# Local attention: the gate projected with its columns on the partitions, two blocks of rows moving

## The chip, the cores and the metric

One Trainium2 chip, one of its cores. The metric is device time in microseconds of one execution, from start to end. Three runs of the kernel before gave 1719.83, 1720.24 and 1720.41 us; the median is 1720.24.

## The reference

One decoder layer on x, 4096 rows of 1024, in float32. One input projection gives the columns of two branches. Branch A is attention over a sliding window of 128 rows with 8 query heads and 2 key heads of 64, a sink per head and partial rotary; branch B is a chunked gated linear attention. Each branch has a gate path.

```python
proj = jnp.einsum('bsd,de->bse', x, w_in[layer])
q_a, k_a, v_a, g_a, q_b, k_b, v_b, g_b, r_b = split_cols(proj, IN_SPLITS)
out_a = sliding_window_attention(q_a, k_a, v_a, attn_sinks[layer]) * jax.nn.silu(g_a)
...
mix = jnp.einsum('bse,ed->bsd', jnp.concatenate([out_a, out_b], axis=-1), w_out[layer])
x = layer_norm(ALPHA * x + mix, ln_g[layer], ln_b[layer])
```

The change is about `silu(g_a)`: 512 gate columns for each row, which multiply branch A's output.

## The kernel before

x is cut into 32 blocks of 128 rows and lies in HBM with its columns first, so that a block in SBUF has 128 of the 1024 columns on the partitions, in eight slices k. Every float32 operand of a product is split into a rounded high part and the low rest (`split`, line 97), and each product is made of three matmuls: high by high, high by low, low by high (`project`, lines 142 to 144). There x is the stationary operand, 128 by 128, and the weights move, up to 512 columns; the result has rows on the partitions.

The program has three stages. Stage A (lines 147 to 485) is the local attention: for each block n the queries `pq`, keys and values `pkv`, the gate `pg`, the scores `psc`, and the output. It keeps two steps under way: in the turn of block n, `a_out(n-1)` is worked off in five pieces between the parts of block n's gate projection. Its output `att` is made with the columns on the partitions, since the next stage wants it so, but the gate has rows there, so `a_out` ends with four transposes of the gate (`tg`, line 430) and a product on VectorE (line 431). The order of the pieces is: `turn(0)` and `turn(1)` (transposes of the probabilities `pt`, split into `hl`, and four selects on GpSimd each, into `p`), `mul(0)`, `mul(1)` (four matmuls `po` each), and the gate's product. In between, `a_turn_k` and `a_turn_q` transpose keys (`tk`) and queries (`tq`). The gate's activation (`a_gate`, line 315) is called after the last piece. Stage B (495 to 770) is the linear attention, and stage C (773 on) the output projection `py` and the layer norm. What A and B make goes through HBM (`mixd`) into C.

x is loaded and split by `load_x` (line 127) one block ahead, on GpSimd (high part) and VectorE (low part). Its tiles `xraw`, `xh` and `xl`, two of each, belong to the pool `xp`, which lives through all stages: stage C uses the same tiles for the rows of `mixd` (`mr`, `mh`, `ml`).

Pools are stacked in SBUF. Those of a stage are given back at its end, and the next stage's pools begin at the same place. Stage B's first pool is `wrb`, three raw weight tiles of 2 KB per partition, used for the output weights in the last block; stage C's first is `c1`, whose first tile, `lg` of 4 KB, lies where the first two of these lay. A tile may be written when all that overlaps it has been read.

Matmul results lie in PSUM banks, two of each tag. The order of each engine's instructions isn't quite the program's: when the program is built, a scheduler goes through each engine's instructions by priority in program order, takes the first whose inputs and tiles are ready by its own estimate of times, and so fills gaps with later work. On the chip each engine then keeps this order, and SyncE's queue of DMA issues too.

The start (lines 150 to 210) loads and splits x of blocks 0 and 1 and the weights of queries, keys and values; the gate's weights follow at line 459, through six raw tiles (`wra`). Blocks 0 and 30 project the queries and keys of two blocks (`both`).

Of the kernel before, what the change touches and what calls it, by code (L numbers as in the profile page):

```python
# [9 lines left out]
F32 = mybir.dt.float32  # L10
F32R = mybir.dt.float32r
# [39 lines left out]
def layer_kernel(  # L51
# [74 lines left out]

    def load_x(n, heng, leng):
        raw = xp.tile([P, NK, P], F32, tag="xraw", name=f"xraw{n}")
        sp.dma_start(raw, xt[n])
        h = xp.tile([P, NK, P], F32R, tag="xh", name=f"xh{n}")  # L130
        l = xp.tile([P, NK, P], F32R, tag="xl", name=f"xl{n}")
        for q in range(2):
            s = slice(4 * q, 4 * q + 4)
            split(h[:, s], l[:, s], raw[:, s], heng, leng)
        return h, l

    def project(dst, x, wg, n, k0=0, k1=NK):

        hs, ls = wg
        for k in range(k0, k1):  # L140
# [3 lines left out]
            pe.matmul(dst[:, :n], b, hs[k][:, :n], start=False, stop=(k == NK - 1))  # L144


    with ExitStack() as pa:
        e1 = pa.enter_context(tc.tile_pool(name="e1", bufs=1))
        wr = pa.enter_context(tc.tile_pool(name="wra", bufs=6))
        with ExitStack() as pstart:  # L150
# [12 lines left out]
            for m in range(2):  # L163
                raws.append(xp.tile([P, NK, P], F32, tag="xraw", name=f"xraw{m}"))
                xs.append(tuple(xp.tile([P, NK, P], F32R, tag=t, name=f"{t}{m}") for t in ("xh", "xl")))
            w = []
            for c in range(4):
                s = slice(2 * c, 2 * c + 2)
                for m in range(2):
                    sp.dma_start(raws[m][:, s], xt[m][:, s])  # L170
                    w.append(load_chunk(ws, w_a, 2 * c + m, 0, 512, 0, 512))
            w += [load_chunk(ws, w_a, k, 512, 256, 1, 272) for k in range(NK)]
            posi = e1.tile([P, NB], I32, tag="posi", name="posi")
            sp.dma_start(posi, pos)
            for c in range(4):
                s = slice(2 * c, 2 * c + 2)
                for m in range(2):
                    split(xs[m][0][:, s], xs[m][1][:, s], raws[m][:, s], act, dve)
                    split(*w[2 * c + m], act, dve)
# [3 lines left out]

            posf = e1.tile([P, NB], F32, tag="posf", name="posf")
            dve.tensor_copy(posf, posi)
            freq = e1.tile([P, HALF], F32, tag="freq", name="freq")
# [4 lines left out]
            ang = e1.tile([P, NB, HALF], F32, tag="ang", name="ang")  # L191
            t1 = e1.tile([P, NB, HALF], F32, tag="t1", name="t1")
            dve.tensor_tensor(
# [104 lines left out]
        def a_turn_q(n, qk):  # L298

            tq = bank("tp", f"tq{n}")  # L300
            for j in range(4):
                pe.transpose(
                    tq[:, j * P : (j + 1) * P],
                    qk[:, 2 * j : 2 * j + 2, :].rearrange("p h d -> p (h d)"),
                    ident,
                )
            qs = e2.tile([P, 8, P], F32R, tag="qs", name=f"qs{n}")
            tqv = tq.rearrange("p (j s) -> p j s", j=4)
            act.copy(qs[:64, :4, :], tqv[:64])
            dve.tensor_tensor(qs[64:, :4, :], tqv[:64], qs[:64, :4, :], ALU.subtract)  # L310
            act.copy(qs[:64, 4:, :], tqv[64:])
            dve.tensor_tensor(qs[64:, 4:, :], tqv[64:], qs[:64, 4:, :], ALU.subtract)
            return qs

        def a_gate(n, pg):
            sg = a2.tile([P, 512], F32, tag="sg", name=f"sg{n}")
            tanh[0] = act.activation(sg, pg, AF.Tanh, scale=0.5)
            dve.scalar_tensor_tensor(sg, sg, 1.0, pg, ALU.add, ALU.mult)
            return sg

        def a_scores(n, qs):
# [13 lines left out]
            for g in range(2):  # L335
# [23 lines left out]
                dve.tensor_tensor(es[:, gs], ngm[:, gs], snk[:, gs], ALU.add)  # L359
                pr = a4.tile([P, 4, P], F32, tag="pr", name=f"pr{n}_{g}")  # L360
                for i in range(4):
# [10 lines left out]

        def a_out(n, pn, sg):

# [61 lines left out]

        scores, sg, wb, qks, kks = None, None, {}, {}, {}
        for n in range(NB):
            last = n == NB - 1
            if 0 < n < NB - 1:  # L440
                xs.append(load_x(n + 1, pool, dve))
            both = n in (0, NB - 2)
            group = [n, n + 1] if both else [] if n in (1, NB - 1) else [n]
            pqs = [bank("pj", f"pq{m}") for m in group]
            for i in range(4):
                for m, pq in zip(group, pqs):
                    project(pq, xs[m], wq, 512, 2 * i, 2 * i + 2)
                if scores:
                    pn = next(scores)
# [12 lines left out]
            if n == 2:  # L462
                wb["k"] = load_group(wr, w_b, 272, 256, 3, 256)
            po = a_out(n - 1, pn, sg) if n > 0 else iter(())
# [4 lines left out]
            project(pg, xs[n], wg, 512, 3, 6)  # L469
            next(po, None)  # L470
            a_turn_k(n, kks[n])
            project(pg, xs[n], wg, 512, 6, 7)
            qs = a_turn_q(n, qks[n])
            project(pg, xs[n], wg, 512, 7, 8)
# [9 lines left out]
        for _ in a_out(NB - 1, pn, sg):  # L484
            pass
# [8 lines left out]

    with ExitStack() as pb:
        wr = pb.enter_context(tc.tile_pool(name="wrb", bufs=3))
        f1 = pb.enter_context(tc.tile_pool(name="f1", bufs=1))
        f2 = pb.enter_context(tc.tile_pool(name="f2", bufs=2))
        b1 = pb.enter_context(tc.tile_pool(name="b1", bufs=1))
        b2 = pb.enter_context(tc.tile_pool(name="b2", bufs=2))  # L500

        am = [b1.tile([P, 4, P], F32, tag=f"am{i}", name=f"am{i}") for i in range(2)]
        qbh = [b1.tile([P, 2, 2, P], F32R, tag=f"qbh{i}", name=f"qbh{i}") for i in range(2)]
# [222 lines left out]
        for n in range(NB):  # L726
            x, last = bx_next, n == NB - 1
            if not last:
                bx_next = load_x(n + 1, pool, dve)
            pq = bank("pj", f"bq{n}")  # L730
# [41 lines left out]

    with ExitStack() as pcx:
        c1 = pcx.enter_context(tc.tile_pool(name="c1", bufs=1))
        c2 = pcx.enter_context(tc.tile_pool(name="c2", bufs=2))
# [4 lines left out]
        for n in range(NB):  # L780
            raw = xp.tile([P, NK, P], F32, tag="xraw", name=f"mr{n}")
            sp.dma_start(raw[:, :4, :], mixd[n][0])
            sp.dma_start(raw[:, 4:, :], mixd[n][1])
            xr = c2.tile([P, D], F32, tag="xr", name=f"xr{n}")
            sp.dma_start(xr, xn[n * P : (n + 1) * P, :])
            mh = xp.tile([P, NK, P], F32R, tag="xh", name=f"mh{n}")
            ml = xp.tile([P, NK, P], F32R, tag="xl", name=f"ml{n}")
            split(mh, ml, raw, act, dve)
            y = c2.tile([P, D], F32, tag="y", name=f"y{n}")
# [108 lines left out]
```

## Time and profile before

| what | value |
|---|---|
| median of 3 runs | 1720.24 us |
| the profiled execution | 1719.78 us |
| its span, first to last instruction | 1718.1 us |
| mean granted TensorE clock | 0.997 |
| DMA, mean over the span | 70 GB/s |

The profile is of one execution of its own. Engines are named PE (TensorE's matmuls), PEld (its weight loads), DVE (VectorE), ACT (ScalarE), POOL (GpSimd) and SP (SyncE). A row gives the line of the kernel, the operation and the tiles it writes and reads (`out<-in`, buffer numbers left out). Matmuls are pipelined: one of 512 columns shows 0.39 us, but the next starts 0.23 us later, so on TensorE starts are compared, not durations. An arrow in brackets says who ended an idle time.

### The profile page before, as it was taken

What the parts mean: (1) busy time and instruction counts of PE and PEld (TensorE: products, weight loads), DVE (VectorE), ACT (ScalarE), POOL (GpSimd) and SP (SyncE); (2) the same over time, 40 slices, a digit from 0 to 9 for tenths busy, and PEclk for the clock granted to TensorE, in tenths of its full rate; (3) what the DMA queues carried; (4) which work ended last, traced back from release to release, by engine and by line L of the source; (5) the groups of instructions that cost most, each with busy time, mean ns of one, the idle gap of its engine ahead of it and who ended that gap; (6) DMA issues with size and microseconds to landing.
All of it is one profiled execution on the core that took longest, in us unless ns stands there. A gap on an engine that the chain in (4) does not pass through costs nothing.

```text
span 1718.1 us, 26157 instructions
## 1 busy us (share of the span) xinstructions
PE 1689.6 (98%) x9477; PEld 1445.5 (84%) x9477; DVE 1123.9 (65%) x2562; ACT 774.8 (45%) x2070; POOL 486.6 (28%) x623
## 2 busy tenths in 40 slices
PE   8999999999999998999999999999999899999998
PEld 7788888888888886888888888888888788888886
DVE  7777777777777786666666666666665755555555
ACT  6444344444344455555555555555555522222221
POOL 1333223333223355222222222222222422222221
PEclk9999999999999999999999999999999999999999
DMA  6211111111111131111111111111111444444442
GB/s 221 70 38 38 48 46 38 38 37 38 49 45 38 38 110 63 45 38 38 38 38 38 38 38 38 38 38 38 38 38 38 154 147 147 145 142 142 148 147 86
DMA packets 66389, 119.68 MB, mean 70 GB/s; under 512 B 22738, under 2 KB 27220, under 8 KB 66260
## 3 DMA queue, kind: packets, MB, share of 16 engines
q1 hardware_dynamic: 66260, 118.01, 21.6%
q8 instruction: 74, 1.21, 0.3%
q14 instruction: 55, 0.45, 0.1%
HBM read 84.37 MB, written 33.62 MB: 69 GB/s over the span
## 4 chain that ended last, share of the span: by engine, by line
PE 58%; DVE 1%; ACT 0%; issue 0%; POOL 0%; DVEq 0%
PE py L142 7%; PE py L144 7%; PE py L143 7%; PE bg L142 3%; PE bg L144 3%; PE bv L142 3%; PE bv L143 3%; PE bg L143 3%; PE bv L144 3%; PE bq L142 2%; PE bq L143 2%; PE bq L144 2%; PE bk L144 2%; PE bk L143 2%; PE bk L142 2%; PE to L719 1%
## 5 line engine op out<-in xcount | busy, mean ns | idle before, releaser
L394 POOL TENSOR_SCALAR_AFFINE_SELECT p<-hl 128x512 fp32r<-128x512 f32 x256 | 165.2, 681 | 385.9 <-ACT hl L388 351.7
L142 PE MATMUL py<-wh,mh 128*128 128x512 f32 x512 | 199.8, 390 | 0.0
L143 PE MATMUL py<-wl,mh 128*128 128x512 f32 x512 | 199.7, 390 | 0.0
L144 PE MATMUL py<-wh,ml 128*128 128x512 f32 x512 | 199.4, 390 | 0.0
L363 ACT ACTIVATE pr<-psc,ngm 128x128 f32<-128x128 f32 x256 | 90.5, 366 | 196.0 <-PE psc L344 138.1
L813 POOL TENSOR_TENSOR y<-y,lg 128x1024 f32<-128x1024 f32 x31 | 74.2, 2392 | 267.9 <-ACT y L812 267.9
L567 POOL TENSOR_TENSOR qp<-bqs,ee 128x256 f32<-128x256 f32 x32 | 23.7, 740 | 337.4 <-ACT ee L564 323.4
L144 PEld LDWEIGHTS py<-wh,ml 128*128 128x128 f32 x512 | 96.4, 188 | 20.1
L143 PEld LDWEIGHTS py<-wl,mh 128*128 128x128 f32 x512 | 96.4, 188 | 19.8
L142 PEld LDWEIGHTS py<-wh,mh 128*128 128x128 f32 x512 | 96.4, 188 | 19.7
L142 PE MATMUL pg<-wh,xh 128*128 128x512 f32 x256 | 110.8, 433 | 1.5 <-ACT wh L100 1.5
L142 PE MATMUL bg<-wh,xh 128*128 128x512 f32 x256 | 107.3, 419 | 0.0
L142 PE MATMUL bv<-wh,xh 128*128 128x512 f32 x256 | 103.8, 405 | 0.0
L100 ACT CAST mh<-mr 128x1024 fp32r<-128x1024 f32 x32 | 33.7, 1053 | 154.2 <-PE py L143 154.2
L142 PE MATMUL pq<-wh,xh 128*128 128x512 f32 x256 | 103.2, 404 | 0.0
L144 PE MATMUL bg<-wh,xl 128*128 128x512 f32 x256 | 101.2, 395 | 0.0
L144 PE MATMUL pg<-wh,xl 128*128 128x512 f32 x256 | 101.0, 395 | 0.0
L144 PE MATMUL pq<-wh,xl 128*128 128x512 f32 x256 | 101.0, 395 | 0.0
L143 PE MATMUL bv<-wl,xh 128*128 128x512 f32 x256 | 101.0, 395 | 0.0
L143 PE MATMUL bg<-wl,xh 128*128 128x512 f32 x256 | 100.8, 394 | 0.0
L143 PE MATMUL pq<-wl,xh 128*128 128x512 f32 x256 | 100.7, 393 | 0.0
L143 PE MATMUL pg<-wl,xh 128*128 128x512 f32 x256 | 100.3, 392 | 0.2 <-DVE wl L105 0.2
(225 smaller groups left out, 4897.1 us busy)
## 6 DMA issues: line engine op xcount, KB each, us to landing
xraw<-in_xt_dram SPq DMA_DIRECT2D x62, 512.0 KB
mr<-mx SPq DMA_DIRECT2D x64, 256.0 KB
xr<-in_xn_dram SPq DMA_DIRECT2D x32, 512.0 KB
out_dram<-y SPq DMA_DIRECT2D x31, 512.0 KB
mx<-att SPq DMA_DIRECT2D x32, 256.0 KB
mx<-mb SPq DMA_DIRECT2D x32, 256.0 KB
wraw<-in_w_a_dram SPq DMA_DIRECT2D x16, 256.0 KB
wraw<-in_w_b_dram SPq DMA_DIRECT2D x16, 256.0 KB
```

What stands on the lines that cost most here:

```text
L100: act.copy(hdst, src)
L142: pe.matmul(dst[:, :n], a, hs[k][:, :n], start=(k == 0), stop=False)
L143: pe.matmul(dst[:, :n], a, ls[k][:, :n], start=False, stop=False)
L144: pe.matmul(dst[:, :n], b, hs[k][:, :n], start=False, stop=(k == NK - 1))
L363: act.activation(pr[:, i], sc[i], AF.Exp, bias=ngm[:, h : h + 1], scale=0.125, accum_out=den[:, h : h + 1])
L394: pool.affine_select(o, hl[:, i], [[0, 4], [sg_, P]], ALU.is_gt if b else ALU.is_ge, 0.0, base=0, channel_multiplier=-sg_,)
L567: pool.tensor_tensor(qp, B[n]["q"], ee, ALU.mult)
L719: pe.transpose(to[:, hs], og[:, hs], ident)
L813: pool.tensor_tensor(y, y, lg, ALU.mult)
```

## The change

Stage A's x is held in tiles of two blocks, so that 256 rows lie side by side. The gate's weights become the stationary operand, 128 columns at a time, and x moves, 256 rows of a pair; the result has the columns on the partitions. The even block of a pair projects gate columns 0 to 255 for both blocks, the odd one the rest. The four transposes go, and the product reads the gate from SBUF. The activation is called before the product. The gate's weights are loaded in two halves of columns. To make room, x's tiles no longer live through all stages: each stage has its own, and only two raw tiles of half a block (`xw`) are common; `wra` has three tiles for six, and some tiles move between pools (`pr`, `qs`, start-up tiles).

```diff
-    xp = ctx.enter_context(tc.tile_pool(name="xp", bufs=2))
+    xw = ctx.enter_context(tc.tile_pool(name="xw", bufs=2))
...
+    def one_block(xp, n):
+        t = xp.tile([P, 2, NK, P], F32R, tag="xhl", name=f"xhl{n}")
+        return t[:, 0], t[:, 1]
+
+    def load_halves(wr, src, c0, slot):
+        hs, ls = ([wp.tile([P, 512], F32R, tag=f"w{t}{slot}_{k}", name=f"w{t}{slot}_{k}") for k in range(NK)] for t in "hl")
+        for i in range(2):
+            c = slice(256 * i, 256 * i + 256)
+            for k in range(0, NK, 2):
+                raw = wr.tile([P, 512], F32, tag="wraw", name=f"wraw{slot}_{k}_{i}")
+                for j in range(2):
+                    r = raw[:, 256 * j : 256 * j + 256]
+                    sp.dma_start(r, src[k + j, :, c0 + 256 * i : c0 + 256 * i + 256])
+                    split(hs[k + j][:, c], ls[k + j][:, c], r, act, dve)
+        return hs, ls
...
-    def load_x(n, heng, leng):
-        raw = xp.tile([P, NK, P], F32, tag="xraw", name=f"xraw{n}")
-        sp.dma_start(raw, xt[n])
-        h = xp.tile([P, NK, P], F32R, tag="xh", name=f"xh{n}")
-        l = xp.tile([P, NK, P], F32R, tag="xl", name=f"xl{n}")
+    def load_x(n, parts, heng, leng):
+        h, l = parts
         for q in range(2):
             s = slice(4 * q, 4 * q + 4)
-            split(h[:, s], l[:, s], raw[:, s], heng, leng)
+            raw = xw.tile([P, 4, P], F32, tag="xraw", name=f"xraw{n}_{q}")
+            sp.dma_start(raw, xt[n][:, s])
+            split(h[:, s], l[:, s], raw, heng, leng)
...
+    def project_turned(dst, x, wg, cols, k0=0, k1=NK):
+        hs, ls = wg
+        for k in range(k0, k1):
+            a, b = (t[:, k].rearrange("p m s -> p (m s)") for t in x)
+            for i, c in enumerate(cols):
+                o = dst[:, 256 * i : 256 * i + 256]
+                c = slice(c * P, (c + 1) * P)
+                pe.matmul(o, hs[k][:, c], a, start=(k == 0 and i == 0), stop=False)
+                pe.matmul(o, hs[k][:, c], b, start=False, stop=False)
+                pe.matmul(o, ls[k][:, c], a, start=False, stop=(k == NK - 1 and i == 1))
...
+        xa = pa.enter_context(tc.tile_pool(name="xa", bufs=2))
+        xpair = []
+        def half_pair(n):
+            if n % 2 == 0:
+                t = xa.tile([P, 2, NK, 2, P], F32R, tag="xhl", name=f"xhl{n}")
+                xpair.extend([(t[:, 0], t[:, 1])] * 2)
+            return tuple(t[:, :, n % 2, :] for t in xpair[n])
-        wr = pa.enter_context(tc.tile_pool(name="wra", bufs=6))
+        wr = pa.enter_context(tc.tile_pool(name="wra", bufs=3))
...
+        sgs = {}
         def a_gate(n, pg):
-            sg = a2.tile([P, 512], F32, tag="sg", name=f"sg{n}")
+            if n % 2 == 0:
+                sgs[n] = sgs[n + 1] = a2.tile([P, 4, 2, P], F32, tag="sg", name=f"sg{n}")
+            sg = sgs[n][:, 2 * (n % 2) : 2 * (n % 2) + 2].rearrange("p j m s -> p (j m s)")
...
-            tg = bank("tp", f"tg{n}")
-            for j in range(4):
-                pe.transpose(tg[:, j * P : (j + 1) * P], sg[:, j * P : (j + 1) * P], ident)
-            dve.scalar_tensor_tensor(att, att, 0.5, tg, ALU.mult, ALU.mult)
+            dve.scalar_tensor_tensor(
+                att.rearrange("p (j s) -> p j s", j=4),
+                att.rearrange("p (j s) -> p j s", j=4),
+                0.5,
+                sgs[n][:, :, n % 2, :],
+                ALU.mult,
+                ALU.mult,
+            )
...
-            if 0 < n < NB - 1:
-                xs.append(load_x(n + 1, pool, dve))
+            for m in (2, 3) if n == 1 else (n + 2,) if 1 < n < NB - 2 else ():
+                xs.append(load_x(m, half_pair(m), pool, dve))
...
-                wg = load_group(wr, w_a, 768, 512, 2, 512, True)
+                wg = load_halves(wr, w_a, 768, 2)
...
+            cols = (0, 1) if n % 2 == 0 else (2, 3)
-            project(pg, xs[n], wg, 512, 0, 3)
+            project_turned(pg, xpair[n], wg, cols, 0, 3)
...
             if last:
-                bx_next = load_x(0, pool, dve)
                 wb["g"] = load_group(wr, w_b, 1040, 512, 2, 512)
+            a_gate(n, pg)
             next(po, None)
-            sg = a_gate(n, pg)
...
     with ExitStack() as pb:
+        xb = pb.enter_context(tc.tile_pool(name="xb", bufs=2))
         wr = pb.enter_context(tc.tile_pool(name="wrb", bufs=3))
...
+        bx_next = load_x(0, one_block(xb, 0), act, dve)
...
     with ExitStack() as pcx:
+        xc = pcx.enter_context(tc.tile_pool(name="xc", bufs=2))
+        c4 = pcx.enter_context(tc.tile_pool(name="c4", bufs=4))
...
-            raw = xp.tile([P, NK, P], F32, tag="xraw", name=f"mr{n}")
-            sp.dma_start(raw[:, :4, :], mixd[n][0])
-            sp.dma_start(raw[:, 4:, :], mixd[n][1])
+            raws = []
+            for q in range(2):
+                raws.append(c4.tile([P, 4, P], F32, tag="mraw", name=f"mr{n}_{q}"))
+                sp.dma_start(raws[q], mixd[n][q])
...
-            split(mh, ml, raw, act, dve)
+            mh, ml = one_block(xc, n)
+            for q in range(2):
+                s = slice(4 * q, 4 * q + 4)
+                split(mh[:, s], ml[:, s], raws[q], act, dve)
```

Two tiles of a pair take 32 KB per partition, two of one block (`xb`, `xc`) 16 KB. So `wrb` begins 16 KB behind the start of stage B's pools, and `c4`, four half tiles of 2 KB, 16 KB behind the start of stage C's.

## Rows read from the trace of the kernel before

**Rows 1.** The page's section 1: busy us (share of span) and instructions of each engine.

```profile
PE 1689.6 (98%) x9477; PEld 1445.5 (84%) x9477; DVE 1123.9 (65%) x2562; ACT 774.8 (45%) x2070; POOL 486.6 (28%) x623
```

**Rows 2.** Windows: length, busy us (instructions) by engine, then PEclk, DMA share, GB/s.

```profile
0.00:60.00 60.00, 53.34 (x269) 42.68 (x270) 46.33 (x111) 36.65 (x97) 13.58 (x36) 1.00 0.61 195
60.00:600.00 540.00, 539.68 (x3102) 461.32 (x3101) 406.17 (x958) 228.75 (x796) 173.74 (x273) 1.00 0.13 40
...
1330.00:1400.00 70.00, 64.54 (x302) 52.57 (x302) 45.41 (x91) 32.05 (x67) 23.94 (x19) 0.95 0.51 158
```

**Rows 3.** Groups by form, TensorE and its weight loads: busy us, mean ns | idle before.

```profile
L142 PE MATMUL pkv<-wh,xh 128*128 128x256 f32 x256 | 71.9, 281 | 0.0
...
L142 PEld LDWEIGHTS pkv<-wh,xh 128*128 128x128 f32 x256 | 48.2, 188 | 0.0
```

**Rows 4.** Timeline, TensorE, one block: start us, us, engine, line, op, out<-in, count.

```profile
303.29 1.24 PE L409 MATMUL po<-p,vv 128*128 128x512 f32 x4
304.37 0.38 PE L293 MATMUL tk<-cs,kk 128*128 128x128 f32 x2
...
306.43 1.08 PE L409 MATMUL po<-p,vv 128*128 128x512 f32 x4
307.35 0.60 PE L430 MATMUL tg<-cs,sg 128*128 128x128 f32 x4
307.70 0.48 PE L142 MATMUL pq<-wh,xh 128*128 128x512 f32 x1
308.02 0.40 PE L143 MATMUL pq<-wl,xh 128*128 128x512 f32 x1
...
315.22 0.28 PE L142 MATMUL pkv<-wh,xh 128*128 128x256 f32 x1
...
318.06 0.60 PE L384 MATMUL pt<-cs,pr 128*128 128x128 f32 x4
...
324.19 0.38 PE L293 MATMUL tk<-cs,kk 128*128 128x128 f32 x2
```

**Rows 5.** Timeline, VectorE, the same block; in brackets the wait ahead and its releaser.

```profile
305.24 0.68 DVE L418 TENSOR_TENSOR att<-po,tmp 64x512 f32<-64x512 f32 x1 [1.96 <-ACT tmp L417]
...
307.25 0.94 DVE L105 TENSOR_TENSOR xl<-xraw,xh 128x512 fp32r<-128x512 f32 x1
...
310.27 0.69 DVE L105 TENSOR_TENSOR xl<-xraw,xh 128x512 fp32r<-128x512 f32 x1
310.99 0.69 DVE L431 SCALAR_TENSOR_TENSOR att<-att,tg 128x512 f32<-128x512 f32 x1
...
315.19 0.16 DVE L367 TENSOR_TENSOR den<-den,es 128x4 f32<-128x4 f32 x1 [0.73 <-ACT es L366]
```

**Rows 6.** Timeline, GpSimd, the same block.

```profile
306.44 1.21 POOL L102 TENSOR_SCALAR xh<-xraw 128x512 fp32r<-128x512 f32 x2
...
322.58 3.57 POOL L394 TENSOR_SCALAR_AFFINE_SELECT p<-hl 128x512 fp32r<-128x512 f32 x6 [1.16 <-DVE hl L389]
```

**Rows 7.** Timeline, TensorE, end of the local attention.

```profile
650.79 0.63 PE L384 MATMUL pt<-cs,pr 128*128 128x128 f32 x4 [2.30 <-DVE pr L369]
```

**Rows 8.** Timeline, SyncE's queue (DMA issues), end of the linear attention.

```profile
1355.24 0.33 SPq L119 DMA_DIRECT2D wraw<-in_w_o_dram  x1
...
1361.45 0.33 SPq L778 DMA_DIRECT2D lg<-in_ln_g_dram  x1
```

**Rows 9.** Timeline, GpSimd and ScalarE, end of the linear attention.

```profile
1359.70 1.72 POOL L105 TENSOR_TENSOR wl<-wraw,wh 128x512 fp32r<-128x512 f32 x1
...
1358.06 0.60 ACT L100 CAST wh<-wraw 128x512 fp32r<-128x512 f32 x1
```

**Rows 10.** Timeline, TensorE, end of the linear attention.

```profile
1353.74 0.40 PE L142 MATMUL py<-wh,mh 128*128 128x512 f32 x1
...
1362.96 0.40 PE L144 MATMUL py<-wh,ml 128*128 128x512 f32 x1
...
1364.82 0.63 PE L142 MATMUL py<-wh,mh 128*128 128x512 f32 x1
```

More of the change, by code (lines that the diff above doesn't have):

```diff
@@ L163, in layer_kernel @@
             for m in range(2):
-                raws.append(xp.tile([P, NK, P], F32, tag="xraw", name=f"xraw{m}"))
-                xs.append(tuple(xp.tile([P, NK, P], F32R, tag=t, name=f"{t}{m}") for t in ("xh", "xl")))
+                xs.append(half_pair(m))
             w = []
@@ L169, in layer_kernel @@
                 for m in range(2):
-                    sp.dma_start(raws[m][:, s], xt[m][:, s])
+                    raws.append(ws.tile([P, 2, P], F32, tag="xr2", name=f"xraw{m}_{c}"))
+                    sp.dma_start(raws[-1], xt[m][:, s])
                     w.append(load_chunk(ws, w_a, 2 * c + m, 0, 512, 0, 512))
             w += [load_chunk(ws, w_a, k, 512, 256, 1, 272) for k in range(NK)]
-            posi = e1.tile([P, NB], I32, tag="posi", name="posi")
+            posi = wz.tile([P, NB], I32, tag="posi", name="posi")
             sp.dma_start(posi, pos)
@@ L177, in layer_kernel @@
                 for m in range(2):
-                    split(xs[m][0][:, s], xs[m][1][:, s], raws[m][:, s], act, dve)
+                    split(xs[m][0][:, s], xs[m][1][:, s], raws[2 * c + m], act, dve)
                     split(*w[2 * c + m], act, dve)
@@ L181, in layer_kernel @@
                 split(h, l, raw, act, dve)
-            posf = e1.tile([P, NB], F32, tag="posf", name="posf")
+            posf = wz.tile([P, NB], F32, tag="posf", name="posf")
             dve.tensor_copy(posf, posi)
-            freq = e1.tile([P, HALF], F32, tag="freq", name="freq")
+            freq = wz.tile([P, HALF], F32, tag="freq", name="freq")
             for i, f in enumerate(INV_FREQ):
@@ L190, in layer_kernel @@
             sinT = e1.tile([P, NB, 2, HALF], F32, tag="sinT", name="sinT")
-            ang = e1.tile([P, NB, HALF], F32, tag="ang", name="ang")
-            t1 = e1.tile([P, NB, HALF], F32, tag="t1", name="t1")
+            ang = wz.tile([P, NB, HALF], F32, tag="ang", name="ang")
+            t1 = wz.tile([P, NB, HALF], F32, tag="t1", name="t1")
             dve.tensor_tensor(
@@ L306, in a_turn_q @@
                 )
-            qs = e2.tile([P, 8, P], F32R, tag="qs", name=f"qs{n}")
+            qs = e1.tile([P, 8, P], F32R, tag="qs", name=f"qs{n}")
             tqv = tq.rearrange("p (j s) -> p j s", j=4)
@@ L359, in a_scores @@
                 dve.tensor_tensor(es[:, gs], ngm[:, gs], snk[:, gs], ALU.add)
-                pr = a4.tile([P, 4, P], F32, tag="pr", name=f"pr{n}_{g}")
+                pr = a2.tile([P, 4, P], F32, tag="pr", name=f"pr{n}_{g}")
                 for i in range(4):
@@ L371, in a_scores, with a_out @@
                 yield pn
-        def a_out(n, pn, sg):
+        def a_out(n, pn):
             att = a1.tile([P, 512], F32, tag="att", name=f"att{n}")
@@ L427, in a_out @@
             yield
-            tg = bank("tp", f"tg{n}")
-            for j in range(4):
-                pe.transpose(tg[:, j * P : (j + 1) * P], sg[:, j * P : (j + 1) * P], ident)
-            dve.scalar_tensor_tensor(att, att, 0.5, tg, ALU.mult, ALU.mult)
+            dve.scalar_tensor_tensor(
[6 more added lines that the diff above has]
+            )
             sp.dma_start(mixd[n][0].rearrange("p a s -> p (a s)"), att)
             yield
-        scores, sg, wb, qks, kks = None, None, {}, {}, {}
+        scores, wb, qks, kks = None, {}, {}, {}
         for n in range(NB):
             last = n == NB - 1
-            if 0 < n < NB - 1:
-                xs.append(load_x(n + 1, pool, dve))
+            for m in (2, 3) if n == 1 else (n + 2,) if 1 < n < NB - 2 else ():
+                xs.append(load_x(m, half_pair(m), pool, dve))
             both = n in (0, NB - 2)
@@ L483, in layer_kernel @@
             pass
-        for _ in a_out(NB - 1, pn, sg):
+        for _ in a_out(NB - 1, pn):
             pass
@@ L728, in layer_kernel @@
             if not last:
[L729 removed]
+                bx_next = load_x(n + 1, one_block(xb, n + 1), pool, dve)
             pq = bank("pj", f"bq{n}")
```

11 lines of the change are left out of this document (4 added, 7 removed).

## The prediction

> **What bounds the kernel now.** I read the page first. TensorE is busy 98% of the span and VectorE 65% [rows 1], which would make every TensorE instruction saved a gain. Busy shares are averages, so I went by stage next: in the local-attention blocks from 60 to 600 us TensorE shows 539.68 of 540 us, while the start has 53.34 of 60 and the step from the linear attention into the output stage 64.54 of 70, at a granted clock of 0.95 [rows 2]. The idle time sits at the seams; the blocks look full.
>
> Then one block in order of time. TensorE: the reader is to look at the four `po` matmuls of the first head group. They run from 303.29 to 304.37, 1.08 us, while the second four, 306.43 to 307.35, take 0.92, which is 0.23 each [rows 4]. The 0.16 us is a wait inside the four, too short to be listed as idle. For what? The last selects that fill `p` start on GpSimd when VectorE's `hl` is there [rows 6], so GpSimd and VectorE are late there, not TensorE.
>
> Following VectorE from the end of those matmuls [rows 5]: it starts at 305.24 when ScalarE's `tmp` is there, and from the split of x at 307.25 to the product with the gate at 310.99 nothing is marked as waiting: split, gate, queries, output, split, product stand in a row, and the scores are behind them. The next wait is 0.73 us for ScalarE's exponentials at 315.19, and these waited for VectorE's maxima. So from `tq` on, VectorE and ScalarE hand the work to each other without a gap that TensorE causes, until `hl`, GpSimd's selects and the next `po`. The loop closes in 324.19 - 304.37 = 19.82 us [rows 4], and TensorE, whose own path is 19.82 - 0.16 = 19.66, waits for it. The transposes that go (`tg`) are on TensorE's path and not on this loop.
>
> **The change part by part.** The sum is made against the profiled execution, 1719.78 us (span 1718.10 and 1.68 around it); the median of the runs is 0.46 higher.
>
> *Transposes that go.* Four per block: 307.35 to 307.70 is 0.35, and the first matmul behind them takes 0.32 (307.70 to 308.02) for 0.23, so 0.44 us of TensorE per block [rows 4].
>
> *The gate on half the columns.* Before, 24 matmuls of 512: 24 x 0.23 = 5.52. After, 48 matmuls of 256. The `pkv` matmuls have that form: 24 of them from 315.22 to 318.06, 0.1183 each [rows 4], so 5.68, +0.16. Their weight loads last 188 ns each [rows 3], longer than the pace, so they overlap. The Trainium skill speaks against the change here: "Perfetto Trace Analysis", Identifying the Most-Contended Engine, takes the weight loads' busy share as TensorE's measure, and 24 loads more per block would then count in full; the `pkv` rows disagree, and this rule gives the last rival below.
>
> TensorE's path of a block comes to 19.66 - 0.44 + 0.16 = 19.38. It can gain at most 19.82 - 19.38 = 0.44, and only where the other loop lets it.
>
> *x by pairs.* Two splits of x on VectorE (0.94 and 0.69) stand in the loop of each block now, because GpSimd's casts start at 306.44, when the gate's last matmul has let go of the old x [rows 5, 6]. With pair tiles, the first block of a pair still waits for that. The second goes into a tile that is already its own, so its splits are ready inside the block before and find VectorE's gaps (0.73 at 315.19). So of two blocks one, without splits, is 1.63 us shorter on VectorE and runs at TensorE's 19.38: -0.44. The other keeps its splits and gets the pair's second casts beside it. Its price isn't in the trace: below, it is -0.44 (its own splits leave too); above, +1.38 (both extra splits, 0.69 each, ahead of the exponentials). I take +0.25, once the difference between 0.94 and 0.69, the same split beside GpSimd's cast and without. 28 blocks (2 to 29) are 14 pairs: 14 x (0.25 - 0.44) = -2.7; ends 14 x -0.88 = -12.3 and 14 x 0.94 = +13.2.
>
> The product with the gate now has both inputs in SBUF instead of one in PSUM. The trace shows no such product beside a GpSimd cast. The Trainium skill, "SBUF — State Buffer", Who interferes with whom, says that a VectorE instruction with two SBUF inputs is blocked by a GpSimd instruction that reads SBUF. The split's 0.94 beside the cast agrees. By that rule the product too could wait out a cast, an estimate of 0.60 (half of 1.21), where my sum has 0.25.
>
> *Order of the gate and the smaller buffers.* The gate's activation moves ahead of the product; on VectorE it stood ahead already, so 0. `pr`, `qs` and `sg` are written after their last reader of the block before, hidden by a whole block: 0; if one of them were late the price would be a part of the 0.16 that exists now.
>
> *Start.* The gate's weights come as two halves, 32 loads for 8, three raw tiles for six; block 0 needs one half. x2 and x3 are loaded together, into free tiles. TensorE idles 6.66 us in the first 60 [rows 2], which is the lower end; the upper is one more load in the way, 1355.24 to 1358.06 or +2.8 [rows 8, 9]. I take -1.0, between them.
>
> *Into the linear attention.* Two gates' transposes go where TensorE was full: -0.9. x for its first block is loaded by a later line, but into the place of a pair that is done since block 29, so the load can start early, hidden under blocks 30 and 31. Ends: -2.3 (the longest wait there goes [rows 7]) and +4.1 (uncovered: load 2.8, cast 0.60, split 0.69).
>
> *Into the output stage.* This is the step that costs. Before, block 0's `mr` was loaded and split long ahead, because it used x's own tiles, and 21 `py` matmuls (1353.74 to 1362.96) filled TensorE's waits at the end of the linear attention; the rest go on at 1364.82 [rows 10]. After, the first `mr` tile lies where stage B's first raw weight tile lay. What that means the trace shows with `lg`, which lies there now: its load is issued at 1361.45, right when the split of the last output weights ends (1359.70 + 1.72) [rows 8, 9]. So `mr` is issued then, lands 2.8 later and is cast in 0.6: first `py` at 1364.9. Lost: 21 x 0.23 = 4.8, and 0.1. The clock was 0.95 of full over these 70 us [rows 2], at two levels 7 us at 1.2 GHz, which cost 3.5; with TensorE emptier I add 0.8. Against it, ScalarE and VectorE have no second `mr` split in that tail; I take -1.0 (a cast of 0.60 and part of its split). Sum +4.7; ends 0 (another tile of the four is given first) and +8.4 (4.9 and the clock's 3.5 again). The steady output stage has the same matmuls: 0. Stage B's splits stay behind a whole block of TensorE work: 0.
>
> Sum: -2.7 - 1.0 - 0.9 + 4.7 = +0.1, so 1719.9 against the profiled execution, 1720.3 as a median.
>
> **Rivals.**
>
> *TensorE is the bound, as the page says.* For it: 98%, and a loop only 0.16 us longer than TensorE's path. It needs the splits to leave the loop in both blocks: 28 x -0.44 = -12.3, with the other terms -9.5: 1710.7. Its near edge is the second block at no price: 14 x -0.44 = -6.2, in all -3.4: 1716.8. Against it: the pair's first tile is still freed by the gate's last matmul.
>
> *The second splits get in the way.* At the place where VectorE waits 0.73 us for the exponentials, a split of 0.69 that meets GpSimd's cast lasts 0.94, and the reciprocals behind it, then `pr`, `hl`, the selects and `po`, are late. One split placed there badly costs the pair 0.94 instead of 0.25: 14 x 0.69 = +9.7 more, 1730.0. It decides for slower from 0.49 us per pair. For it: the order on VectorE is fixed at build time by estimates. Against it: the gap is as long as the undisturbed split.
>
> *The change doesn't do what it says: the loads set the pace.* 48 loads of 188 ns instead of a pace of 0.1183 are +3.34 us per block, 32 times +107: 1827. Against it: 24 `pkv` matmuls in a row that keep their pace.
>
> **How the numbers follow.** No change that can be told (within 0.2%, 3.4 us, about what a measurement of this kernel can tell): 0.36. TensorE bound, faster: 0.32. Second splits in the way, or the output stage's price at its upper end, slower: 0.31. Loads set the pace: 0.01. Faster 0.32, same 0.36, slower 0.32. The likeliest gives 1720.3, its own range 1716.9 to 1723.7. The range takes in most of both neighbours: 1711 to 1729; what is left out are the far ends of the steady term.
>
> **What would show it.** Right: no `tg`, and gate matmuls of 256 at 0.118; blocks in pairs, one near 19.4 us and one near 20.1; waits of TensorE before `po` or `pt` in the second kind; no `py` before the last output weights are split, and `mr` issued with that split. Wrong: a steady pitch near 19.4 in all blocks (the first rival), one above 19.9 on average (the second), or `py` still filling the tail at 1353 to 1363.

## The result: 0.9% slower, and the profile after

The changed kernel takes 1736.95 us (median of 6 runs, 1732.96 to 1739.68), the kernel before 1720.93 beside it (6 runs); the ratio is 1.009, 95% interval [1.0077, 1.0104]. The forecast was 1720.3, no change that can be told; the time lies 8 us above the range's end of 1729. The profiled execution took 1738.01 us, with a span of 1736.2.

Six stretches of the span, cut where TensorE starts the same operation in both kernels (`tq` of blocks 2 and 29, `tb`, a transpose of the linear attention, of blocks 1 and 30, `py` of block 2), show where the time went. The marks are starts of matmuls in the two traces; the forecast of -2.7 was made for 28 blocks:

| stretch | before, us | after, us | change | forecast |
|---|---|---|---|---|
| start, to block 2 | 67.47 | 70.04 | +2.57 | -1.0 |
| 27 blocks of local attention | 535.05 | 539.44 | +4.38 | -2.7 |
| into linear attention | 95.85 | 101.15 | +5.30 | -0.9 |
| linear attention | 625.39 | 624.14 | -1.26 | 0 |
| into the output stage | 59.51 | 66.19 | +6.68 | +4.7 |
| output stage | 334.79 | 335.20 | +0.41 | 0 |

Section 1 of the page after, against [rows 1]: TensorE has 640 matmuls more and the same busy time, since four transposes went per block and 24 matmuls of 512 became 48 of 256.

```profile
PE 1689.7 (97%) x10117; PEld 1482.4 (85%) x10117; DVE 1121.0 (65%) x2602; ACT 784.1 (45%) x2112; POOL 492.3 (28%) x621
```

The windows after, with the columns of [rows 2]: TensorE is no longer full between 60 and 600, and the granted clock is below full wherever it idles more, in the start, into the linear attention (a window of 80 us) and into the output stage.

```profile
0.00:60.00 60.00, 52.13 (x294) 44.68 (x295) 45.08 (x110) 35.81 (x94) 17.80 (x40) 0.94 0.58 177
60.00:600.00 540.00, 530.78 (x3617) 484.15 (x3617) 403.81 (x956) 231.15 (x792) 174.88 (x268) 1.00 0.12 41
600.00:680.00 80.00, 70.58 (x432) 59.58 (x432) 56.96 (x127) 43.45 (x129) 36.31 (x46) 0.94 0.31 90
1330.00:1400.00 70.00, 58.99 (x291) 48.58 (x290) 41.41 (x82) 34.41 (x76) 22.13 (x19) 0.90 0.42 136
```

The blocks do come in pairs. Here are the starts of `tq` on TensorE: a short block of 19.40 (309.50 to 328.90) and a long one of 20.78 (to 349.68).

```profile
309.50 0.60 PE L340 MATMUL tq<-cs,qk 128*128 128x128 f32 x4
...
328.90 0.60 PE L340 MATMUL tq<-cs,qk 128*128 128x128 f32 x4
...
349.68 0.60 PE L340 MATMUL tq<-cs,qk 128*128 128x128 f32 x4
```

Of the 27 intervals 14 are short (19.40 to 19.43). Of the 13 long ones nine take 20.76 to 20.80, three 19.93 to 19.98, and one 20.94: there the last x split comes late, because its cast waits for the load.

```profile
498.59 0.62 POOL L102 TENSOR_SCALAR xhl<-xraw 128x512 fp32r<-128x512 f32 x1 [3.42 <-DMA xraw<-in_xt_dram]
```

Why there are two kinds of long block shows on VectorE. First the long block of above. All four x splits (L105) stand in it; the first takes 1.08, the gate's product (L470) 1.10 and the negated maximum (L400), which four exponentials wait for, 0.57: it ends at 338.38, and the cast beside it (below) at 338.37.

```profile
330.96 1.08 DVE L105 TENSOR_TENSOR xhl<-xraw,xhl 128x512 fp32r<-128x512 f32 x1
...
334.13 0.69 DVE L105 TENSOR_TENSOR xhl<-xraw,xhl 128x512 fp32r<-128x512 f32 x1
334.74 1.10 DVE L470 SCALAR_TENSOR_TENSOR att<-att,sg 128x512 f32<-128x512 f32 x1
...
337.21 0.68 DVE L105 TENSOR_TENSOR xhl<-xraw,xhl 128x512 fp32r<-128x512 f32 x1
337.81 0.57 DVE L400 SCALAR_TENSOR_TENSOR ngm<-mx,nsnk 128x4 f32<-128x4 f32 x1
...
338.71 0.68 DVE L105 TENSOR_TENSOR xhl<-xraw,xhl 128x512 fp32r<-128x512 f32 x1
```

GpSimd in the same block: each of the three long operations has a cast of x beside it that started first (the second of the pair at 330.31, then 334.69 and 337.45).

```profile
330.31 1.21 POOL L102 TENSOR_SCALAR xhl<-xraw 128x512 fp32r<-128x512 f32 x2 [0.34 <-PE pg L172]
334.69 0.62 POOL L102 TENSOR_SCALAR xhl<-xraw 128x512 fp32r<-128x512 f32 x1 [3.17 <-DMA xraw<-in_xt_dram]
337.45 0.92 POOL L102 TENSOR_SCALAR xhl<-xraw 128x512 fp32r<-128x512 f32 x1 [2.14 <-DMA xraw<-in_xt_dram]
```

Now a long block of the other kind (210.02 to 229.95, 19.93), VectorE and then GpSimd. The product starts 0.10 ahead of the cast and takes 0.68; it is the cast that takes 1.07 instead of 0.62, and the maximum, clear of the next cast, takes 0.15.

```profile
215.86 0.68 DVE L470 SCALAR_TENSOR_TENSOR att<-att,sg 128x512 f32<-128x512 f32 x1
...
218.51 0.15 DVE L400 SCALAR_TENSOR_TENSOR ngm<-mx,nsnk 128x4 f32<-128x4 f32 x1
```

```profile
215.96 1.07 POOL L102 TENSOR_SCALAR xhl<-xraw 128x512 fp32r<-128x512 f32 x1 [3.32 <-DMA xraw<-in_xt_dram]
218.72 0.62 POOL L102 TENSOR_SCALAR xhl<-xraw 128x512 fp32r<-128x512 f32 x1 [1.70 <-DMA xraw<-in_xt_dram]
```

The same instructions in the same order differ by 0.42 in the product and 0.42 in the maximum, and the blocks by 0.85. Which engine comes first, by 0.05 in one block and 0.10 in the other, decides. The Trainium skill, "SBUF — State Buffer", Who interferes with whom, has the rule: a VectorE instruction with two SBUF inputs contends with a GpSimd instruction that reads SBUF, and issue order decides who blocks. These rows agree in both directions (the product 1.10 behind the cast, the cast 1.07 behind the product).

At the seams: the first `py` comes at 1375.88, behind a `mr` that is issued at 1371.20; GpSimd's last split of the output weights ended at 1371.17 (1369.46 + 1.71). GpSimd, SyncE's queue, TensorE:

```profile
1369.46 1.71 POOL L105 TENSOR_TENSOR wl<-wraw,wh 128x512 fp32r<-128x512 f32 x1
...
1371.20 0.80 SPq L834 DMA_DIRECT2D mr<-mx  x2
...
1375.88 0.80 PE L158 MATMUL py<-wh,xhl 128*128 128x512 f32 x1 [1.10 <-ACT xhl L100]
```

In the 5.5 us behind, the granted clock was 0.50, the lower of its two levels (the window's columns as above), after five waits of 1.0 to 1.7 us on TensorE between 1364 and 1376.

```profile
1376.00:1381.50 5.50, 5.50 (x13) 4.34 (x14) 4.14 (x12) 1.89 (x5) 0.00 (x0) 0.50 0.81 285
```

Into the linear attention, the first x is cast on ScalarE only at 662.66, though the local attention's last gate matmul started at 649.58, and its first `bq` matmul starts at 663.33. Its load had been issued at 578.34. In the kernel before, `bq` filled TensorE's waits from 642.90 on. ScalarE, TensorE:

```profile
662.66 0.61 ACT L100 CAST xhl<-xraw 128x512 fp32r<-128x512 f32 x1
...
663.33 0.39 PE L158 MATMUL bq<-wh,xhl 128*128 128x272 f32 x1 [0.51 <-ACT xhl L100]
```

### The profile page after: what moved, and what is told of

The parts are those of the page before. It is cut to its first block, busy times and chain, and to the rows that moved or that the text cites. A ratio compares the mean times of both kernels' runs of the same rounds, so it can differ in the third digit from the quotient of the medians.

```text
span 1736.2 us, 27711 instructions
## 1 busy us (share of the span) xinstructions
PE 1689.7 (97%) x10117; PEld 1482.4 (85%) x10117; DVE 1121.0 (65%) x2602; ACT 784.1 (45%) x2112; POOL 492.3 (28%) x621
## 4 chain that ended last, share of the span: by engine, by line
PE 80%; DVE 9%; ACT 3%; DMA 3%; POOL 3%; issue 2%; SPq 0%; DVEq 0%; ACTq 0%; POOLq 0%
PE py L158 7%; PE py L159 7%; PE py L160 7%; PE bv L158 3%; PE bv L159 3%; PE bv L160 3%; PE bg L158 3%; PE bg L159 3%; PE bg L160 3%; PE po L451 3%; PE pg L172 3%; PE pg L170 3%; PE pg L171 3%; ACT pr L405 2%; DVE xhl L105 2%
## 5 line engine op out<-in xcount | busy, mean ns | idle before, releaser
L158 PE MATMUL py<-wh,xhl 128*128 128x512 f32 x512 | 200.5, 392 | 1.1 <-ACT xhl L100 1.1
L159 PE MATMUL py<-wl,xhl 128*128 128x512 f32 x512 | 200.5, 392 | 0.0
L160 PE MATMUL py<-wh,xhl 128*128 128x512 f32 x512 | 199.9, 391 | 0.0
L170 PE MATMUL pg<-xhl,wh 128*128 128x256 f32 x512 | 154.8, 302 | 2.2 <-ACT wh L100 1.8
L172 PE MATMUL pg<-xhl,wl 128*128 128x256 f32 x512 | 145.4, 284 | 0.0
L171 PE MATMUL pg<-xhl,wh 128*128 128x256 f32 x512 | 145.2, 284 | 0.0
L158 PEld LDWEIGHTS py<-wh,xhl 128*128 128x128 f32 x512 | 96.8, 189 | 21.7 <-ACT xhl L100 1.4
L160 PEld LDWEIGHTS py<-wh,xhl 128*128 128x128 f32 x512 | 96.7, 189 | 20.0
L158 PE MATMUL bg<-wh,xhl 128*128 128x512 f32 x256 | 106.8, 417 | 1.7 <-ACT pr L405 1.7
L105 DVE TENSOR_TENSOR xhl<-xraw,xhl 128x512 fp32r<-128x512 f32 (+1 forms) x132 | 100.8, 781 | 7.3 <-POOL xhl L102 2.7
L158 PE MATMUL bv<-wh,xhl 128*128 128x512 f32 x256 | 103.4, 404 | 0.0
L158 PE MATMUL pq<-wh,xhl 128*128 128x512 f32 x256 | 101.3, 396 | 0.0
L159 PE MATMUL pq<-wl,xhl 128*128 128x512 f32 x256 | 101.1, 395 | 0.1
```

Source lines behind the costliest of these rows:

```text
L105: leng.tensor_tensor(ldst, src, hdst, ALU.subtract)
L158: pe.matmul(dst[:, :n], a, hs[k][:, :n], start=(k == 0), stop=False)
L159: pe.matmul(dst[:, :n], a, ls[k][:, :n], start=False, stop=False)
L170: pe.matmul(o, hs[k][:, c], a, start=(k == 0 and i == 0), stop=False)
L171: pe.matmul(o, hs[k][:, c], b, start=False, stop=False)
L172: pe.matmul(o, ls[k][:, c], a, start=False, stop=(k == NK - 1 and i == 1))
```

## Experiments

Each is compared with the kernel before, run on the same chip, and read by the stretches (of one profile each):

| kernel | median, us | ratio, 95% | start | 27 blocks | into linear | linear | into output | output |
|---|---|---|---|---|---|---|---|---|
| e1_hold | 1725.86 | 1.0034 [1.0021, 1.0047] | 66.18 | 530.65 | 100.60 | 623.87 | 66.52 | 334.95 |
| e2_act | 1719.84 | 1.0001 [0.9991, 1.0010] | 66.33 | 524.51 | 101.45 | 623.82 | 66.22 | 335.23 |
| e3_mr | 1729.04 | 1.0055 [1.0040, 1.0070] | 69.80 | 537.68 | 101.59 | 624.09 | 59.71 | 334.95 |
| e4_seam | 1731.13 | 1.0068 [1.0053, 1.0083] | 68.01 | 537.12 | 97.33 | 623.75 | 66.31 | 334.93 |
| e5_notg | 1714.09 | 0.9956 [0.9942, 0.9971] | 68.48 | 528.30 | 95.85 | 625.35 | 58.39 | 334.78 |
| e6_bact | 1714.71 | 0.9963 [0.9948, 0.9977] | 65.45 | 530.63 | 95.89 | 625.40 | 59.75 | 334.78 |
| e7_all | 1706.75 | 0.9916 [0.9901, 0.9930] | 65.70 | 524.30 | 96.75 | 624.23 | 58.72 | 334.71 |
| e8_idle | 1721.58 | 1.0004 [0.9994, 1.0013] | 67.04 | 524.83 | 102.90 | 623.93 | 66.43 | 334.60 |
| e9_beside | 1721.95 | 1.0015 [1.0005, 1.0025] | 68.70 | 524.71 | 101.16 | 624.07 | 66.77 | 335.34 |

**e1_hold: the second splits one step later.**

```diff
-            for m in (2, 3) if n == 1 else (n + 2,) if 1 < n < NB - 2 else ():
+            if n == 1 or n % 2 == 0 and 1 < n < NB - 2:
+                m = 2 * (n // 2) + 2
                 xs.append(load_x(m, half_pair(m), pool, dve))
+            behind = hold.get("pool")
...
+            if n % 2 and n < NB - 2:
+                with ExitStack() as late:
+                    late.enter_context(tc.issue_after(hold["dve"]))
+                    if behind is not None:
+                        late.enter_context(tc.issue_after(behind))
+                    xs.append(load_x(n + 2, half_pair(n + 2), pool, dve))
```

`hold` keeps the last of VectorE's low parts of the probabilities and the last select on GpSimd; the new lines stand behind `a_out`'s second `turn`.

> The changed kernel, with the x splits of a pair's second block held back by one step: on VectorE they are issued behind the low part of the probabilities, on GpSimd behind the selects of the step before. Theory (the second splits stand before the exponentials of the block that follows, and their casts slow VectorE beside them): the long blocks fall from 20.77 us to 19.8 or less, the short ones stay within 19.4 to 19.7, because two splits of 0.68 fit into VectorE's wait of 2.38 ahead of the output's sum; a pair takes 39.0 to 39.6 in place of 40.17, the steady stretch from block 2 to block 29 (539.4) 525 to 533, and the time is 1721 to 1731. Rival 1 (it is the amount of VectorE's work, wherever it stands): the short blocks take over what the long ones lose, a pair stays at 40.0 to 40.3 and the time at 1735 to 1739. Rival 2 (the long blocks wait for the pair's tile, not for the second splits): they stay at 20.7.

The 27 blocks fell from 539.44 to 530.65, nearer to the theory, and rivals 1 and 2 are out: short blocks stay at 19.40 (one 19.55), though two splits now stand in them. But most long blocks are of two kinds, 19.5 and 19.9 (two of the 13 are longer, 20.4 and 21.0), and again VectorE's split and GpSimd's pair of casts tell why. Here is a block of 19.52, VectorE and GpSimd, and then one of 19.97:

```profile
126.70 0.69 DVE L105 TENSOR_TENSOR xhl<-xraw,xhl 128x512 fp32r<-128x512 f32 x1
...
126.04 1.83 POOL L102 TENSOR_SCALAR xhl<-xraw 128x512 fp32r<-128x512 f32 x2
```

```profile
165.62 1.14 DVE L105 TENSOR_TENSOR xhl<-xraw,xhl 128x512 fp32r<-128x512 f32 x1
...
164.97 1.25 POOL L102 TENSOR_SCALAR xhl<-xraw 128x512 fp32r<-128x512 f32 x2
```

The casts take 1.83 and the split 0.69, or the casts 1.25 and the split 1.14: one engine waits, and only VectorE's wait costs the block, 0.45 for 0.45.

**e2_act: the casts on ScalarE.**

```diff
-                xs.append(load_x(m, half_pair(m), pool, dve))
+                xs.append(load_x(m, half_pair(m), act, dve))
```

> The changed kernel, with the high parts of x in the local attention made on ScalarE, not GpSimd; VectorE's splits are as many as before. If GpSimd's casts slow VectorE beside them (product 1.10 against 0.69 us, the negated maximum 0.57 against 0.16, the split 1.08 against 0.69), these three are back at 0.69, 0.16 and 0.69, and the long blocks fall from 20.77 to 19.9 to 20.3; a pair takes 39.3 to 39.7 and the time is 1723 to 1731. If only the number of splits counts, the three rows fall as well but the long blocks stay at 20.5 or more, and the time is 1734 to 1739; ScalarE's casts of 0.62 could also stand before the exponentials and give the same.

More than expected: all blocks but two (19.17 and 20.34) take 19.40, long or short alike, with all four splits still in every second one. VectorE in such a block (318.30 to 337.70):

```profile
320.88 0.69 DVE L105 TENSOR_TENSOR xhl<-xraw,xhl 128x512 fp32r<-128x512 f32 x1
...
323.05 0.69 DVE L105 TENSOR_TENSOR xhl<-xraw,xhl 128x512 fp32r<-128x512 f32 x1
323.66 0.68 DVE L470 SCALAR_TENSOR_TENSOR att<-att,sg 128x512 f32<-128x512 f32 x1
...
325.71 0.68 DVE L105 TENSOR_TENSOR xhl<-xraw,xhl 128x512 fp32r<-128x512 f32 x1
326.31 0.15 DVE L400 SCALAR_TENSOR_TENSOR ngm<-mx,nsnk 128x4 f32<-128x4 f32 x1
...
329.26 0.16 DVE L400 SCALAR_TENSOR_TENSOR ngm<-mx,nsnk 128x4 f32<-128x4 f32 x1
329.34 0.69 DVE L411 TENSOR_TENSOR pr<-pr,rec 128x512 f32<-128x512 f32 x1
```

So the number of splits is no cost. The casts on GpSimd are: 0.40, 0.42 and 0.42 on split, product and maximum, 1.24 of the 1.37 between 20.77 and 19.40. (In the block of 20.34 the last split waits for its load, as in that of 20.94 before.) Not all is shown by this run, since the build also ordered VectorE a little otherwise: here the second maximum stands ahead of the product `pr`, in the changed kernel behind it. The start gives back 3.7 too, but not all of that is the casts'. Up to 600 us e4, below, has the instructions of the changed kernel in the same order on VectorE, ScalarE and GpSimd, and its start takes 68.01 in place of 70.04; the granted clock from 20 to 60 was 1.00 in e4 and e2 and 0.91 in the changed kernel. Windows of 20 to 60 in the changed kernel, e4 and e2:

```profile
20.00:60.00 40.00, 34.33 (x219) 30.22 (x219) 30.80 (x77) 22.90 (x66) 15.43 (x20) 0.91 0.52 153
20.00:60.00 40.00, 33.99 (x237) 29.79 (x236) 32.16 (x80) 22.90 (x66) 16.07 (x20) 1.00 0.58 169
20.00:60.00 40.00, 36.49 (x258) 32.31 (x257) 32.84 (x87) 29.32 (x86) 8.87 (x12) 1.00 0.55 160
```

**e3_mr: `mr` in free tiles**, and **e4_seam: x split a turn earlier.**

```diff
-                raws.append(c4.tile([P, 4, P], F32, tag="mraw", name=f"mr{n}_{q}"))
+                p, t = (xw, "xraw") if n == 0 else (c4, "mraw")
+                raws.append(p.tile([P, 4, P], F32, tag=t, name=f"mr{n}_{q}"))
```

> The changed kernel, with the first block of the output stage loaded into the two raw x tiles (free since the last x split) in place of tiles that lie on the weights' raw tiles of the stage before. Theory (the load waits for the last weight split, so 21 matmuls of the output projection no longer fill the end of the linear attention): its load is issued near 1335 in place of 1371, the stretch from the linear attention's block 30 to the output's block 2 falls from 66.2 to 59 to 61 us, all others stay, and the time is 1730 to 1732. Rival (the second half of the weights, split on GpSimd, sets it): the load is early, the stretch stays above 64 and the time at 1735 or more.

```diff
             if last:
+                seam = tc.cur_priority
...
-        xb = pb.enter_context(tc.tile_pool(name="xb", bufs=2))
+        xb = pb.enter_context(tc.tile_pool(name="xb", bufs=2, reuse_waits="tile"))
...
-        bx_next = load_x(0, one_block(xb, 0), act, dve)
+        with tc.high_priority(tc.cur_priority - seam):
+            bx_next = load_x(0, one_block(xb, 0), pool, dve)
```

> The changed kernel, with the first x block of the linear attention split in the last turn of the local attention (its tile waits only for the pair that lay there, and its instructions are placed where the kernel before had them), again on GpSimd and VectorE. Theory (its q projection no longer fills the last turns): the stretch from block 29's queries to the linear attention's block 1 falls from 101.2 to 95 to 97 us, all others stay, and the time is 1731 to 1733. Rival (the gate's activation, which now stands before the last output piece, is what lengthens it): the stretch stays above 99.5 and the time at 1735 or more.

Both theories hold. e3: `mr` is issued at 1315.63, even before the expected 1335, the first `py` starts at 1363.55, right behind the last matmul of the block's state (`pu`, 1363.43), and the stretch falls by 6.48. SyncE's queue, TensorE:

```profile
1315.63 0.92 SPq L835 DMA_DIRECT2D mr<-mx  x2
...
1363.55 0.40 PE L158 MATMUL py<-wh,xhl 128*128 128x512 f32 x1
```

e4: the first `bq` starts at 648.42, and the stretch falls by 3.8 to 97.33, a little over the range. The 1.5 left to the kernel before may be the clock: from 640 to 660 it was 0.83 here and 1.00 before, which is at most 3.4 us; this wasn't tried. The edit changes three things at once, the place in the order, what the tile waits for and the engine of the cast, so which of them had held the cast is not shown. TensorE, and the window (columns of [rows 2]):

```profile
648.42 0.39 PE L158 MATMUL bq<-wh,xhl 128*128 128x272 f32 x1 [1.70 <-POOL xhl L102]
```

```profile
640.00:660.00 20.00, 16.04 (x94) 14.21 (x94) 15.97 (x31) 12.25 (x35) 14.77 (x16) 0.83 0.51 159
```

The two runs also repeat the blocks of the changed kernel, which neither edits. Of their 26 long blocks 13 have a product of 1.10 to 1.14 and a maximum of 0.57 and take 20.74 to 20.79; eleven have 0.68 to 0.69 and 0.15 to 0.16 and take 19.92 to 20.03; in the other two the last split is late. How many go which way differs from one execution to the next: the 27 blocks took 539.44, 537.68 and 537.12 in the three profiles. The time of e3, 1 us under its range, may be that.

**e5_notg: the kernel before without the gate's transposes**, and **e6_bact: the kernel before with its casts on ScalarE.**

The first leaves the gate unturned, so its output is another one.

```diff
-            tg = bank("tp", f"tg{n}")
-            for j in range(4):
-                pe.transpose(tg[:, j * P : (j + 1) * P], sg[:, j * P : (j + 1) * P], ident)
-            dve.scalar_tensor_tensor(att, att, 0.5, tg, ALU.mult, ALU.mult)
+            dve.scalar_tensor_tensor(att, att, 0.5, sg, ALU.mult, ALU.mult)
```

> The kernel before, without the four transposes of the gate: the product takes the gate as it lies in SBUF, with rows on the partitions, so what is multiplied is left unturned. It tests the prediction's first step alone. If the steady block of before is bound by the loop through VectorE, ScalarE and GpSimd, taking 0.44 us from TensorE changes little: the block stays at 19.7 to 19.85 us and the time at 1717 to 1721. If TensorE bounds it, the block falls to 19.38 and the time to 1705 to 1709.

```diff
-                xs.append(load_x(n + 1, pool, dve))
+                xs.append(load_x(n + 1, act, dve))
```

> The kernel before, with the high parts of x in the local attention made on ScalarE, not GpSimd, as in e2_act. If the casts on GpSimd also lengthen the loop of before, its block falls from 19.82 to TensorE's own path of 19.66, the steady stretch by 4 to 5 us and the time to 1714 to 1717: then of e2_act's gain over the changed kernel only the rest belongs to the pairs. If they cost before nothing, it stays at 19.82 and 1719 to 1721.

e5 lies between its two cases: the block falls from 19.82 to 19.57, so of the 0.44 on TensorE 0.25 came through. The loop through VectorE was not quite separate from the transposes (how they meet wasn't tried apart; the product had waited for them). e6 hits: 19.65, TensorE's own path as read from [rows 4] (19.66). The casts on GpSimd cost the kernel before 0.16 per block as well.

**e7_all: e2, e3 and e4 together**, no other edit.

> The changed kernel with e2_act, e3_mr and e4_seam together. If the three causes are separate, the stretches are those measured one by one: 66.3 to the steady blocks, 524.5 in them, 97 into the linear attention, 623.8 in it, 59.7 into the output stage, 335 to the end; with 1.7 around the span 1706 to 1710 us, faster than before by 0.6 to 0.8%. If the seams' gains depend on what ScalarE does, it is 1712 or more.

1706.75, ratio 0.9916 [0.9901, 0.9930]: faster than the kernel before by 14 us. The stretches are those of the single edits within 1.0 us, so the three causes are separate. Against e6, which has the ScalarE casts but not the change, it is 8.0 faster, 6.3 of it in the 27 blocks (19.40 in place of 19.65 in all but two): this is what the change is worth in the blocks where nothing hides it.

**e8_idle and e9_beside: the contention put back on e2.** They missed their aim. The first lines are e8's, in `load_x`, the others e9's, in `a_gate`.

```diff
+            if idle is not None:
+                for i in range(2):
+                    pool.tensor_scalar(idle, raw[:, 2 * i : 2 * i + 2], 1.0, 1.0, ALU.mult, ALU.mult)
...
+            for i in range(8):
+                pool.tensor_scalar(idle, sg[:, 256 * (i % 2) : 256 * (i % 2) + 256], 1.0, 1.0, ALU.mult, ALU.mult)
```

> e2_act with the casts on GpSimd added back as work that nobody uses: each half block of x is also copied on GpSimd into a tile that is never read (two of 128x256 for each cast of before); ScalarE still makes the high parts. Theory (GpSimd's reads slow VectorE's operations with two SBUF operands beside them): the product takes 1.1 us again in the long blocks, these are back at 20.0 to 20.8 us, and the time is 1727 to 1737. Rival (VectorE and TensorE waited for the casts' results, or for their place in GpSimd's queue ahead of the selects): nothing waits for these copies, blocks stay at 19.4 and the time at 1719 to 1722.

> e2_act (x cast on ScalarE, every block at 19.40 us) with GpSimd work put where the casts of the changed kernel hurt: once a block's gate is ready, GpSimd copies it eight times (128x256 each, some 2.5 us together) into a tile that nobody reads, so that copies run while VectorE makes the gate's product and, in the long blocks, the x split before it. No instruction waits for them. Theory (VectorE's operations with two SBUF operands take about 0.41 longer beside GpSimd's reads, and on the way to the exponentials that lengthens the block): the product or the split before it takes 1.1 in place of 0.69, the short blocks keep 19.4, since they have room ahead of the exponentials, the long ones take 19.7 to 20.3, and the time is 1723 to 1731. Rival (only waiting for the casts' results counted): all blocks stay at 19.4 and the time at 1719 to 1722.

In e8 the copies came later than the casts of the changed kernel and did not meet the product (0.68 to 0.69), but in eleven of 13 long blocks the last split, 0.90 to 0.93; blocks stay at 19.40 to 19.53 (but for the first, and one of 20.31, as in e2). In e9 they did meet product and split, but cost 0.19 and 0.10, VectorE:

```profile
325.44 0.79 DVE L105 TENSOR_TENSOR xhl<-xraw,xhl 128x512 fp32r<-128x512 f32 x1
326.16 0.88 DVE L473 SCALAR_TENSOR_TENSOR att<-att,sg 128x512 f32<-128x512 f32 x1
```

and the blocks keep 19.40 (but for the first and one of 20.52). So the rival's times came out, though not for its reason in e9, where VectorE was slowed. Both runs show that e2's long block has room. A long block ends 8.06 us behind its second maximum wherever VectorE sets its length (19.51 with a maximum 11.45 behind `tq` and 19.92 with 11.85 in e1; 19.93 with 11.87 and 20.77 with 12.70 in the changed kernel); in e9 it comes at 10.8 to 11.2 (12.47 in the block of 20.52), which makes 19.3 at most, below TensorE's 19.40. That each conflict lengthens a block rests on the two kinds of block within one trace (changed kernel, e1, and the repeats in e3 and e4), not on these two runs.

## Why the prediction was wrong, point by point

- *What bounds the kernel before.* Mostly right: TensorE's own path is 19.66 (e6: 19.65) and the rest a loop outside of it. What made the loop late by 0.16 was not read: GpSimd's casts.
- *Transposes and turned gate.* Right. The short block takes 19.40 for 19.38, and loads of 192 ns (median, 188 in [rows 3]) don't set the pace: the gate's matmuls start 0.12 apart. That the transposes are not on the loop was too strong (e5: 0.25 of 0.44 came through). The order of the gate and the smaller buffers, put at 0, cost nothing that shows: e2's blocks, with both, take 19.40.
- *x by pairs: the step that failed.* "I take +0.25, once the difference between 0.94 and 0.69, the same split beside GpSimd's cast and without." Against 19.82 the long block costs 0.97 more in ten of 13 and 0.13 in three, 0.78 on average over all: 14 x -0.41 and 10.1 make the stretch's +4.4. I counted one conflict of 0.25 where in nine of them three of 0.40 to 0.42 stand in a row ahead of the exponentials, 1.24 together. The product's was named in the prediction, 0.60 by the Trainium skill's rule ("SBUF — State Buffer", Who interferes with whom), and left out of the sum; it is 0.42. The average block of 19.98 is the sign that the prediction gave for its second rival, and that rival's size (0.94) was right, but by luck, since its mechanism was wrong: the extra splits themselves cost nothing (e2), and what stood badly was the maximum beside a cast, ahead of the exponentials and not the reciprocals behind them.
- *Start*, -1.0 for +2.57. Two things show: the granted clock (0.91 from 20 to 60; e4, at 1.00, takes 68.01 with the same instructions, +0.54 against before) and the casts (e2, at 1.00 too, takes 66.33). The gain of 1.0 didn't come: like against like, with the casts on ScalarE in both, the changed kernel's start is 0.88 longer than that of before (e2, e6). The loads of the gate's weights are 16, not 32 as the prediction counted; what they cost wasn't tried.
- *Into the linear attention*, -0.9 for +5.30: a second step that failed. The load did start early, at 578.34, as forecast; I took its cast and split to be early with it. The cast comes at 662.66, behind the local attention's last turn, and TensorE lost its filler (e4: 3.8 of it, with another clock) and the full clock, 0.94 granted in the window of 80 us and 1.00 before, which is 4.8 us at most.
- *Into the output stage*, +4.7 for +6.68. The mechanism was right to the instruction (`mr` on the weights' tile, issued when the last split ends, no `py` before it; e3 gives back 6.48). The size was off by 2.0. Twelve of the first `py` started 0.43 apart and not 0.23, at 1.2 GHz, and four before, so on these alone the clock costs 1.6 more, where I had 0.8. The rest, and with it whether the credit of 1.0 for the second `mr` split came, isn't resolved.
- *Linear attention*, 0 for -1.26 (a block takes 21.51 in place of 21.57): not tried.

The sum was +0.1 for 18.1 in the span. Of the 18.0 between them 7.1 lie in the blocks, 3.6 in the start, 6.2 and 2.0 at the seams and -0.9 elsewhere. All four terms of the sum came out high, together by 18.9, and the range had room for 8.7. They are related: the casts on GpSimd stand in the blocks and in the start, and each seam lost a filler that the kernel before had by its pools' lifetime, and full clock with it.

## What to carry to other kernels

Before moving work between engines or blocks, list which VectorE operations with two SBUF operands will stand beside GpSimd's reads on the path that binds, and price each (0.40 to 0.45 here), not once. When a pool's place or lifetime changes, follow the first tile of each new stage to what lay there and when its last reader ends, and look at which engine's written order its first use falls into: the two fillers at the seams, with the clock that went with them, were worth 3.8 and 6.5 us here. If the timeline shows the same instruction with two durations, compare the blocks with the one and the other: it is an experiment that has been run already.

## What the runs showed of the hardware that was not expected

A VectorE operation on 4 elements per partition, 0.16 us alone, takes 0.57 beside a GpSimd cast: it ends with the cast (338.38 and 338.37), and loses as much as one of 512 elements (0.41 and 0.42). The wait goes to whoever is second by as little as 0.05 to 0.1 us, and that turned a block of 19.93 into one of 20.77 in nine cases of 13, with the same instructions. Beside copies of 128x256 the wait was 0.10 to 0.24 (e8, e9) in place of 0.4.
